# An S5, gMLP and attention layer on one core: the taps of all octaves ahead of the scan

## The chip, the cores and the metric

The kernel runs on one core of one Trainium2 chip. The metric is the device time of one execution in microseconds (us). Before the change three runs took 903.1, 904.47 and 906.89 us; their median, 904.47, is "the time before".

## The reference, cut to what matters

One encoder layer on 512 tokens of 1024 features: two mixers side by side (an S5 state space and a gMLP with spatial gating), merged by sigmoid gates, then cross-attention to 256 memory tokens, then a SwiGLU feed-forward part. The change touches the S5 branch alone:

```python
u = xa.reshape(seq, 32 groups, 16 channels)
y = d * u
for direction, reverse in ((0, False), (1, True)):
    lam_bar = exp(lam * step)                       # (32 groups, 64 states), complex
    bu = einsum('gpc,lgc->lgp', b_bar, u)
    states = scan(s[l] = lam_bar * s[l-1] + bu[l])  # over 512 positions
    y += einsum('gcp,lgp->lgc', c, states).real
y = gelu(y)
ya = y * sigmoid(y @ w_glu)
...
merged = gate_a * (ya @ w_proj_a) + gate_b * (yb @ w_proj_b)
```

## The kernel before, in words

**Main stream.** TensorE runs one product after another. Every weight block is loaded by SP (tile `wraw`, some blocks ahead of use), then split into two parts by ScalarE (`whi`, L85) and VectorE (`wlo`, L86), and each product is made of three partial ones. In order: the first half of zv (`tokm`), xa for S5 (`feat`), the second half of zv, gate A, the spatial mixing (`sv`), zu, gate B, then fourteen products with `w_proj_b` in the form of a 2x2 scheme with seven products for each half of the columns (tiles `bx`, `bq`, `qv`, L1193 to L1228), and then `finish_side()`, the GLU product of S5 (`w_glu`, four blocks deep, tile `pf`), `w_proj_a`, `w_out` and the rest. Sums of weight blocks that the 2x2 schemes need are made by DMA in DRAM: SP copies a block (L274), POOL adds another onto it (L275; tiles `bsum`, `qsum`, `dsum`).

**S5 as a side program.** `s5_program` (L955) is a Python generator that issues S5's instructions between those of the main stream. After each weight block the main stream calls `tick(us)` with the block's nominal time (5.2 us for a block of `w_in`, 2.7 for a pair product). A tick adds 0.8 of that time to a credit; while there is credit the generator is run on, and each `yield x` uses up x of it. `yield None` gives the credit back and waits for the next tick. `later(n, f)` has f issued n units of 5.2 us later. So the program order is paced by ticks. Which instruction an engine takes next is then settled by the framework's scheduler, in program order as far as data and buffers are ready; it may bring an instruction forward a long way. Instructions given to `in_order` keep their order among themselves. At run time every engine works its list strictly in order.

**What S5 computes.** The 512 positions are cut into 64 chunks of Q = 8, the 32 groups into four *octaves* of 8.
- `s5_setup` makes powers of lam_bar (`pe`, `pw`, `ca`, `cb`) and the scaled b and c (`raw_c`).
- `s5_kernels(o)` (L781) makes the *factors* of octave o, e0 and e1 (c times powers; 128 x 1024 numbers each; six VectorE operations, L790 to L797), then from them the *taps* inside a chunk: `products` fills `bd` (L804, L807) and multiplies (`pk`, L814, L819), `store` copies them to `ks` (L829) and adds d (L830), `spill` writes them to DRAM (`kd`, L837, L838), and `load` reads them back in Toeplitz form with eight DMAs (`tt`, L845). The factors have two buffers for each of e0 and e1, and tt has one.
- `s5_inputs(o)` (L853) makes the input factors in `wsx` on VectorE, turns them (`pw`), multiplies them with u (`pz`) and keeps the result in `zh` (L878, L879).
- `s5_scan` (L895) runs the recurrence over 62 chunks on VectorE, four small operations a step (L900 to L903).
- `s5_outputs(o)` (L906) copies the shifted states to `ss` (POOL memsets L916 and L917, ScalarE copies L918 and L919, the lower and the upper half of the partitions, for the real and the imaginary part apart), multiplies u with tt and ss with e0 and e1 (`mix_`, tile `py`, L929), copies the sum to `y` (`emit`), turns it (`turn_y`, `pyt`), applies gelu (`put`, L947) and stores y to DRAM (`yd`, L950): one half of the partitions through SP's queue and the other through POOL's.

**The order around the change.** `s5_program` runs the setup, the factors and taps of octaves 0 and 1, the four inputs, the scan, and then outputs 0, factors and taps 2, outputs 1, factors and taps 3, outputs 2, outputs 3. `ks` and `y` share one buffer (tag "y"). At the end `finish_side()` (L1229) issues what is left, the S5 pool is closed (L1230) and a pool `merge` takes its memory. In it lie `ygt`, which reads the four yd back (L1240), and the operands `yg_hi` and `yg_lo` of the GLU product (L1241); `pad` (L130) and the loads of gate A (`gat`, L1263) come there too.

Of the kernel before, what the change touches and what calls it, by code (L numbers as in the profile page):

```python
# [9 lines left out]
F32 = mybir.dt.float32  # L10
# [7 lines left out]
P = 128  # L18
# [8 lines left out]
G = 32  # L27
C = 16
# [11 lines left out]
Q = 8  # L40
NCH = T // Q
NO = 4
GO = G // NO
# [9 lines left out]
def hybrid_layer_kernel(  # L53
# [8 lines left out]
    nc = tc.nc  # L62
# [9 lines left out]
    dp = ctx.enter_context(tc.tile_pool(name="scratch", bufs=1, space=DRAM))  # L72
# [370 lines left out]
    def later(n, fn):  # L443

        side["later"].append((side["now"] + n, fn))
# [103 lines left out]
    s5p = s5.enter_context(tc.tile_pool(name="s5", bufs=1))  # L549
# [47 lines left out]
    ss = row_sums(xt[:, 1, :])  # L597
    for t in range(1, NT):
        rms_scale(xt[:, t, :], g_mix, xt[:, t, :], ss)
        if t == 1:  # L600
            ss = row_sums(xt[:, 2, :])
# [4 lines left out]
        if t == 2:  # L606
            ss = ss3
# [8 lines left out]
    st = {}  # L616
    V = nc.vector
    lo_, hi_ = slice(0, 64), slice(64, 128)

    def s5_setup():  # L620
# [13 lines left out]
        for i, src in enumerate((s5_lam_re, s5_lam_im)):  # L634
# [3 lines left out]
            l = small()  # L638
# [15 lines left out]
        for n in range(2):  # L654
# [2 lines left out]
                nc.tensor.transpose(ps[:, k, :], rows[:, :, 8 * n + k], ident[:2 * G, :2 * G])  # L657
            A_.copy(bb.rearrange("p i g c -> p c (i g)")[:, 8 * n:8 * n + 8, :], ps)
            yield None
        cc = s5p.tile([P, 2, G, C], F32, name="raw_c")  # L660
        for i in range(2):
            ps = aux("pbc", (P, C // 4, P))
            for k in range(C // 4):
# [7 lines left out]
        stp, a, rho, th, n, sn, hs, cs = (small() for _ in range(8))  # L671
# [106 lines left out]
    def glc(t):  # L778
        return t.rearrange("p g a b -> p (g a b)")

    def s5_kernels(o):  # L781

        gs = slice(o * GO, (o + 1) * GO)
        cr, ci = st["c"]
        pr, pi = st["pe"]
        es = []
        for i in range(2):
            e = s5p.tile([P, GO, Q, C], F32, tag="e%d" % i, name="e%d" % i, bufs=2)
            w = s5p.tile([P, GO, Q, C], F32, tag="etmp", name="etmp")
            V.tensor_tensor(e, outer(cr, gs, Q), inner((pr, pi)[i], gs, C), ALU.mult)  # L790
            yield 1.1
            V.tensor_tensor(w, outer(ci, gs, Q), inner((pi, pr)[i], gs, C), ALU.mult)
            yield 1.1
            if i == 0:
                V.tensor_tensor(e, e, w, ALU.subtract)
            else:
                V.scalar_tensor_tensor(glc(e), glc(e), -1.0, glc(w), ALU.mult, ALU.subtract)  # L797
            es.append(e)
            yield 1.1
        def products():  # L800
            bd = []
            for i in range(2):
                t = s5p.tile([P, GO, 2, C], F32, tag="bd", name="bd", bufs=2)
                nc.gpsimd.memset(t, 0.0)  # L804
                for d in range(2):
                    hf = slice(64 * d, 64 * d + 64)
                    nc.scalar.copy(t[hf, :, d, :], st["b"][i][hf, gs, :])  # L807
                bd.append(t)
            ps = aux("pk", (P, 2, P))
            for q in range(2):  # L810
                for i in range(2):
                    for j in range(4):
                        g = 4 * q + j
                        in_order(nc.tensor.matmul(ps[32 * j:32 * j + 32, q, :], bd[i][:, g].rearrange("p d c -> p (d c)"),  # L814
                                                  lc(es[i], g), start=(i == 0), stop=False, tile_position=(0, 32 * j)))
                for i in range(2):
                    for j in range(4):
                        g = 4 * q + j
                        in_order(nc.tensor.matmul(ps[32 * j:32 * j + C, q, 0:C], bd[i][:, g, 1, :],  # L819
                                                  es[i][:, g, Q - 1, :], start=False, stop=(i == 1),  # L820
                                                  tile_position=(0, 32 * j)))
            later(0.5, lambda: store(ps))

        def store(ps):
            ks = s5p.tile([P, 2, P], F32, tag="y", name="ks")
            dd = s5p.tile([P, 2, C], F32, tag="dd", name="dd", bufs=2)
            in_order(V.tensor_tensor(dd, st["dmask"].unsqueeze(1).to_broadcast([P, 2, C]),
                                     st["dcol"][:, 2 * o:2 * o + 2].unsqueeze(2).to_broadcast([P, 2, C]), ALU.mult))
            nc.scalar.copy(ks, ps)  # L829
            V.tensor_tensor(ks[:, :, 0:C], ks[:, :, 0:C], dd, ALU.add)  # L830
            later(0.5, lambda: spill(ks))

        def spill(ks):
            kd = dp.tile([GO, C, 15, C], F32, name=f"kd{o}")
            for j in range(4):
                kdj = kd.rearrange("(q j) c l e -> j c q (l e)", j=4)[j]
                (nc.gpsimd, nc.sync)[o > 1].dma_start(kdj[:, :, 7 * C:15 * C], ks[32 * j:32 * j + C])  # L837
                nc.gpsimd.dma_start(kdj[:, :, 0:7 * C], ks[32 * j + C:32 * j + 2 * C, :, 0:7 * C])  # L838
            later(1.2, lambda: load(kd))

        def load(kd):
            tt = s5p.tile([P, GO, P], F32, tag="tt", name="tt")
            kf = kd.rearrange("g c l e -> c g (l e)")
            for l in range(Q):
                (nc.gpsimd, nc.sync)[o > 1].dma_start(tt[l::Q], kf[:, :, (7 - l) * C:(15 - l) * C])  # L845
            st["oct", o] = (es[0], es[1], tt)

        later(1, products)
        yield 0.1

    turned = set()

# [53 lines left out]
    def s5_outputs(o):  # L906
        gs = slice(o * GO, (o + 1) * GO)
        while ("oct", o) not in st:
            yield None
        e_re, e_im, tt = st["oct", o]  # L910
        zh, u = st["zh"], st["u"]
        ss = s5p.tile([P, 2, GO, NCH], F32, tag="wt", name="ss", bufs=2)
        ss = (ss[:, 0], ss[:, 1])
        for i, s in enumerate(ss):
            zv = zh[:, :, i, gs].rearrange("p n g -> p g n")
            nc.gpsimd.memset(s[lo_, :, 0:1], 0.0)  # L916
            nc.gpsimd.memset(s[hi_, :, NCH - 1:NCH], 0.0)  # L917
            nc.scalar.copy(s[lo_, :, 1:NCH], zv[lo_, :, 0:NCH - 1])  # L918
            nc.scalar.copy(s[hi_, :, 0:NCH - 1], zv[hi_, :, 0:NCH - 1][:, :, ::-1])  # L919

        def mix_():
            ps = aux("py", (P, 4, 2, 4, C))
            for h in range(4):
                for k in range(3):
                    for j in range(2):
                        g = 4 * j + h
                        a = u[:, o * GO + g, :] if k == 0 else ss[k - 1][:, g, :]
                        b = (tt[:, g, :], lc(e_re, g), lc(e_im, g))[k]
                        in_order(nc.tensor.matmul(ps[64 * j:64 * j + 64, :, :, h, :].rearrange("p q d c -> p d q c"), a,  # L929
                                                  b.rearrange("p (d q c) -> p d q c", d=2, q=4),  # L930
                                                  start=k == 0, stop=k == 2, tile_position=(0, 64 * j)))
            later(1, lambda: emit(ps))

        def emit(ps):

            y = s5p.tile([P, 512], F32, tag="y", name="y")
            nc.scalar.copy(y, ps.rearrange("p q d g c -> p (q d g c)"))
            later(0.5, lambda: turn_y(y))

        def turn_y(y):  # L940
            ps = aux("pyt", (P, 2, 4, NCH))
            for q in range(4):
                in_order(nc.tensor.transpose(ps[:, :, q, :], y[:, q * P:(q + 1) * P], ident))
            later(0.5, lambda: put(y, ps))

        def put(y, ps):
            nc.scalar.activation(y, ps.rearrange("p s q n -> p (s q n)"), AF.Gelu_apprx_tanh)  # L947
            ydo = yd[o].rearrange("(s f) (d q) n -> d f s (q n)", s=2, d=2)
            for d in range(2):
                (nc.sync, nc.gpsimd)[d].dma_start(ydo[d], y[64 * d:64 * d + 64].rearrange("p (s r) -> p s r", s=2))  # L950

        later(0.5, mix_)
        yield 0.1

    def s5_program():  # L955
        yield from s5_setup()
        yield from s5_kernels(0)
        yield from s5_kernels(1)
        while "u" not in st:
            yield None  # L960
        zh = s5p.tile([P, NCH, 2, G], F32, name="zh")
        st["zh"] = zh
        for o in range(NO):
            yield from s5_inputs(o)
        while st.get("nz", 0) < 2 * NO:
            yield None
        yield None
        yield from s5_scan()
        for _ in range(2):
            yield None  # L970
        for o in range(NO):
            yield from s5_outputs(o)
            if o + 2 < NO:
                yield from s5_kernels(o + 2)

    def finish_side():
        while side["gen"] is not None or side["later"]:
# [25 lines left out]
    u = s5p.tile([P, G, NCH], F32, tag="u", name="u")  # L1003
# [179 lines left out]
    for q, ts in ((5, T1), (6, T0)):  # L1183
        for i in range(2):
            k = slice(2 * i, 2 * i + 2)
# [641 lines left out]
```

## Time and profile before

| | |
|---|---|
| three runs, median (lowest, highest) | 904.47 us (903.1, 906.89) |
| the profiled execution, its own time | 905.0 us |
| its span, first to last instruction | 903.2 us |
| mean granted clock of TensorE | 0.985 |
| TensorE busy | 867.9 us, 96% |
| VectorE, ScalarE, POOL busy | 643.8, 486.0, 102.2 us |
| HBM | 157.61 MB read, 46.63 MB written |

How to read the lines further down. A wait line names the engine and line that waited, what it waited for, and the total, the number and the longest wait in us. A line of the chain gives the start, the duration and the work that the end hung on. A windows line gives a stretch, its length, each engine's busy time in it (with the instructions), the granted clock (PEclk, 1.00 is full), the busy share of the DMA engines and GB/s. A time line's row gives start, duration, engine, line, operation, output<-input and shape, and in brackets the idle time ahead of it with what ended it. A group's row gives the count and min/median/max in ns, or the busy time in us and the mean in ns. A DMA row gives the count, the size of one and the median us from issue to landing. "SPq" and "POOLq" are those engines as issuers of DMAs.

### The profile page before, as it was taken

How to read it: one execution, taken by the hardware profiler on the slowest of the kernel's cores; microseconds unless marked ns; L12 is line 12 of the kernel's file. 1: busy time of each engine (PE TensorE's matmuls, PEld its weight loads, DVE VectorE, ACT ScalarE, POOL GpSimd, SP SyncE). 2: the span in 40 equal slices, each digit the busy share in tenths (PEclk: the TensorE clock that was granted, in tenths of full speed). 3: DMA queues.
4: the chain of work that ended last, by engine and by line, in shares of the span. 5: the costliest groups of instructions: out<-in, count | busy, mean ns of one | idle time of the engine just before them, and what ended most of it. 6: DMA issues, size and time to landing. Idle time of an engine off the chain costs nothing.

```text
span 903.2 us, 14797 instructions
## 1 busy us (share of the span) xinstructions
PE 867.9 (96%) x5760; PEld 771.5 (85%) x5760; DVE 643.8 (71%) x1048; ACT 486.0 (54%) x716; POOL 102.2 (11%) x153
## 2 busy tenths in 40 slices
PE   9999999999996939999999999999999999999996
PEld 6788888888796828889989978999999999988875
DVE  5698545898585435758856845776778777899875
ACT  5646974343585323446656634655554554665664
POOL 1005201111021110001001101101111111000010
PEclk9999999999998969999999999999999999999999
DMA  8677367878334794663469738428799999356672
GB/s 260 185 207 200 92 191 187 195 181 197 104 95 137 233 260 116 224 207 116 162 207 283 193 115 209 141 54 228 168 258 234 216 226 251 95 163 208 200 229 98
DMA packets 116360, 165.36 MB, mean 183 GB/s; under 512 B 9393, under 2 KB 82241, under 8 KB 116162
## 3 DMA queue, kind: packets, MB, share of 16 engines
q1 hardware_dynamic: 95746, 135.74, 46.3%
q0 software_dynamic: 20256, 28.15, 19.3%
q8 instruction: 45, 0.74, 0.3%
q10 hardware_dynamic: 288, 0.52, 0.2%
q14 instruction: 25, 0.20, 0.1%
HBM read 157.61 MB, written 46.63 MB: 226 GB/s over the span
## 4 chain that ended last, share of the span: by engine, by line
PE 88%; DMA 5%; ACT 3%; issue 2%; DVE 1%; SPq 1%; POOLq 0%; POOL 0%; ACTq 0%; DVEq 0%
PE pf L358 25%; PE pt L358 17%; PE px L1128 12%; PE pq L1128 6%; PE dx L358 5%; PE dq L358 3%; PE pv L1128 3%; PE qx L1128 2%; PE bx L1128 2%; PE dv L358 2%; PE pz L873 2%; DMA yd<-y 1%; PE psc L358 1%; PE qq L1128 1%; PE ptr L520 1%
## 5 line engine op out<-in xcount | busy, mean ns | idle before, releaser
L86 DVE TENSOR_TENSOR wlo<-wraw,whi 128x1024 fp32r<-128x1024 f32 (+1 forms) x145 | 172.3, 1189 | 94.9 <-ACT whi L85 91.1
L85 ACT CAST whi<-wraw 128x1024 fp32r<-128x1024 f32 (+1 forms) x145 | 148.4, 1026 | 155.6 <-PE pf L358 43.9
L358 PE MATMUL pf<-xn,whi 128*128 128x512 f32 x448 | 139.3, 392 | 0.0
L358 PEld LDWEIGHTS pf<-xn,whi 128*128 128x128 f32 x448 | 83.5, 188 | 17.2 <-issue 0.3
L358 PE MATMUL pf<-xn,wlo 128*128 128x512 f32 x224 | 87.4, 390 | 0.0
L1128 PE MATMUL px<-fn,whi 128*128 128x256 f32 x480 | 83.3, 277 | 0.0
L1128 PEld LDWEIGHTS px<-fn,whi 128*128 128x128 f32 x480 | 72.5, 188 | 0.2
L85 ACT CAST whi<-b 128x1024 fp32r<-128x1024 f32 x40 | 42.2, 1054 | 50.7 <-PE px L1128 27.7
L86 DVE TENSOR_TENSOR wlo<-b,whi 128x1024 fp32r<-128x1024 f32 x40 | 48.9, 1223 | 27.3 <-ACT whi L85 27.3
L1128 PE MATMUL px<-fn,wlo 128*128 128x256 f32 x240 | 66.4, 277 | 0.0
L1128 PE MATMUL pq<-s,whi 128*128 128x256 f32 x320 | 55.0, 276 | 0.0
L358 PE MATMUL dx<-whi,s 128*128 128x512 f32 x170 | 53.4, 391 | 0.4 <-DVE h L1752 0.4
L85 ACT CAST whi<-t 128x1024 fp32r<-128x1024 f32 x30 | 31.6, 1054 | 35.3 <-PE pv L1128 12.4
L86 DVE TENSOR_TENSOR wlo<-t,whi 128x1024 fp32r<-128x1024 f32 x30 | 36.7, 1225 | 19.4 <-ACT whi L85 19.4
L358 PEld LDWEIGHTS pf<-xn,wlo 128*128 128x128 f32 x224 | 42.0, 188 | 8.9 <-issue 0.2
L1128 PEld LDWEIGHTS pq<-s,whi 128*128 128x128 f32 x320 | 48.2, 188 | 0.0
L1128 PEld LDWEIGHTS px<-fn,wlo 128*128 128x128 f32 x240 | 45.1, 188 | 0.0
L1128 PE MATMUL pq<-s,wlo 128*128 128x256 f32 x160 | 44.2, 276 | 0.0
L358 PE MATMUL pt<-whi,xn 128*128 128x512 f32 x128 | 43.5, 410 | 0.4 <-ACT xn L85 0.4
L358 PEld LDWEIGHTS dx<-whi,s 128*128 128x128 f32 x170 | 31.8, 188 | 7.5 <-issue 0.8
L275 POOL DMA_DIRECT2D dsum<-in_w_down_dram x12 | 13.2, 1103 | 177.0 <-DMA dsum<-in_w_down_dram 176.6
L358 PE MATMUL dx<-wlo,s 128*128 128x512 f32 x85 | 33.0, 391 | 0.2 <-DVE wlo L86 0.2
(454 smaller groups left out, 2237.9 us busy)
## 6 DMA issues: line engine op xcount, KB each, us to landing
wraw<-in_w_in_dram SPq DMA_DIRECT2D x36, 512.0 KB, 4.5
dsum<-in_w_down_dram SPq DMA_DIRECT2D x20, 512.0 KB, 5.1
wraw<-dsum SPq DMA_DIRECT2D x20, 512.0 KB, 4.2
b<-in_w_gate_dram SPq DMA_DIRECT2D x15, 512.0 KB, 5.2
b<-in_w_up_dram SPq DMA_DIRECT2D x15, 512.0 KB, 4.6
wraw<-in_w_down_dram SPq DMA_DIRECT2D x15, 512.0 KB, 4.2
dsum<-in_w_down_dram POOLq DMA_DIRECT2D x10, 512.0 KB, 7.0
dsum<-dsum POOLq DMA_DIRECT2D x10, 512.0 KB, 7.4
```

The lines of the kernel that those rows point to most:

```text
L85: hi = nc.scalar.copy(dst_hi, src)
L86: lo = nc.vector.tensor_tensor(dst_lo, src, dst_hi.bitcast(F32), ALU.subtract)
L275: plan[j + step][1].append((0, lambda d=dst, x=more: nc.gpsimd.dma_start(d, x, accum_op=ALU.add)))
L358: m = nc.tensor.matmul(ps, a[x], b[y], start=start and i == 0, stop=stop and i == 2, skip_group_check=free)
L520: nc.tensor.transpose(ps[:, j, :], src[:, k * P:(k + 1) * P], ident)
L873: nc.tensor.matmul(ps[:, g, :], wt[:, g, :], u[:, o * GO + g, :], start=True, stop=True)
L1128: nc.tensor.matmul(ps[:, j, :], a[x], b[y], start=start and j == k == i == 0, stop=k == 3 and i == 2, skip_group_check=True)
```

## The change

Taps of all four octaves are made ahead of the scan: `s5_program` makes octaves 2 and 3 where 0 and 1 were, and 0 and 1 after the inputs. As there are two buffers for the factors, those of octaves 2 and 3 are stored to DRAM (`ed`) and read back by `reload`, half a unit after the mix whose buffer they take. `tt` alternates between two buffers, one of them that of `raw_c`. `ks` moves from y's buffer to that of `bd`. All kd stores of the first kind, all tt loads and both halves of y go through SP's queue. The copies to `ss` become one on ScalarE and one on VectorE; the mix begins with e0 and e1 and ends with tt; it is issued one unit after the copies and not half a unit, and each output uses 5.0 of credit and not 0.1.

```diff
-        cc = s5p.tile([P, 2, G, C], F32, name="raw_c")
+        cc = s5p.tile([P, 2, G, C], F32, tag="raw_c", name="raw_c")
...
         def products():
+            if o in ed:
+                for i in range(2):
+                    nc.sync.dma_start(ed[o][i], glc(es[i]))
...
         def store(ps):
-            ks = s5p.tile([P, 2, P], F32, tag="y", name="ks")
+            ks = s5p.tile([P, 2, P], F32, tag="bd", name="ks", bufs=2)
...
-                (nc.gpsimd, nc.sync)[o > 1].dma_start(kdj[:, :, 7 * C:15 * C], ks[32 * j:32 * j + C])
+                nc.sync.dma_start(kdj[:, :, 7 * C:15 * C], ks[32 * j:32 * j + C])
                 nc.gpsimd.dma_start(kdj[:, :, 0:7 * C], ks[32 * j + C:32 * j + 2 * C, :, 0:7 * C])
-            later(1.2, lambda: load(kd))
-
-        def load(kd):
-            tt = s5p.tile([P, GO, P], F32, tag="tt", name="tt")
-            kf = kd.rearrange("g c l e -> c g (l e)")
-            for l in range(Q):
-                (nc.gpsimd, nc.sync)[o > 1].dma_start(tt[l::Q], kf[:, :, (7 - l) * C:(15 - l) * C])
-            st["oct", o] = (es[0], es[1], tt)
+            st["kd", o] = kd
+            if o not in ed:
+                later(1.2, lambda: load(o, es))
...
+    ed = {o: dp.tile([2, P, GO * Q * C], F32, name=f"ed{o}") for o in (2, 3)}
+
+    def load(o, es):
+        tt = s5p.tile([P, GO, P], F32, tag=("tt", "raw_c")[o % 2], name="tt")
+        kf = st["kd", o].rearrange("g c l e -> c g (l e)")
+        for l in range(Q):
+            nc.sync.dma_start(tt[l::Q], kf[:, :, (7 - l) * C:(15 - l) * C])
+        st["oct", o] = (es[0], es[1], tt)
+
+    def reload(o):
+        es = [s5p.tile([P, GO, Q, C], F32, tag="e%d" % i, name="e%d" % i, bufs=2) for i in range(2)]
+        for i, e in enumerate(es):
+            nc.sync.dma_start(glc(e), ed[o][i])
+        load(o, es)
...
-        ss = (ss[:, 0], ss[:, 1])
-        for i, s in enumerate(ss):
-            zv = zh[:, :, i, gs].rearrange("p n g -> p g n")
-            nc.gpsimd.memset(s[lo_, :, 0:1], 0.0)
-            nc.gpsimd.memset(s[hi_, :, NCH - 1:NCH], 0.0)
-            nc.scalar.copy(s[lo_, :, 1:NCH], zv[lo_, :, 0:NCH - 1])
-            nc.scalar.copy(s[hi_, :, 0:NCH - 1], zv[hi_, :, 0:NCH - 1][:, :, ::-1])
+        zv = zh[:, :, :, gs].rearrange("p n i g -> p i g n")
+        nc.gpsimd.memset(ss[lo_, :, :, 0:1], 0.0)
+        nc.gpsimd.memset(ss[hi_, :, :, NCH - 1:NCH], 0.0)
+        nc.scalar.copy(ss[lo_, :, :, 1:NCH], zv[lo_, :, :, 0:NCH - 1])
+        V.tensor_copy(ss[hi_, :, :, 0:NCH - 1], zv[hi_, :, :, 0:NCH - 1][:, :, :, ::-1])
...
-                for k in range(3):
+                for k in (1, 2, 0):
...
-                                                  start=k == 0, stop=k == 2, tile_position=(0, 64 * j)))
+                                                  start=k == 1, stop=k == 0, tile_position=(0, 64 * j)))
             later(1, lambda: emit(ps))
+            if o + 2 in ed:
+                later(0.5, lambda: reload(o + 2))
...
-                (nc.sync, nc.gpsimd)[d].dma_start(ydo[d], y[64 * d:64 * d + 64].rearrange("p (s r) -> p s r", s=2))
-
-        later(0.5, mix_)
-        yield 0.1
+                nc.sync.dma_start(ydo[d], y[64 * d:64 * d + 64].rearrange("p (s r) -> p s r", s=2))
+
+        later(1, mix_)
+        yield 5.0
...
         yield from s5_setup()
-        yield from s5_kernels(0)
-        yield from s5_kernels(1)
+        for o in (2, 3):
+            yield from s5_kernels(o)
...
         for o in range(NO):
             yield from s5_inputs(o)
+        for o in (0, 1):
+            yield from s5_kernels(o)
...
         for o in range(NO):
             yield from s5_outputs(o)
-            if o + 2 < NO:
-                yield from s5_kernels(o + 2)
```

More of the change, by code (lines that the diff above doesn't have):

```diff
@@ L923, in mix_ @@
             for h in range(4):
-                for k in range(3):
+                for k in (1, 2, 0):
                     for j in range(2):
                         g = 4 * j + h
-                        a = u[:, o * GO + g, :] if k == 0 else ss[k - 1][:, g, :]
+                        a = u[:, o * GO + g, :] if k == 0 else ss[:, k - 1, g, :]
                         b = (tt[:, g, :], lc(e_re, g), lc(e_im, g))[k]
```

## The prediction

> **What bounds the kernel now.** I read the page's totals first, then the list of what TensorE waited for, then the chain that ended last around the largest wait, then the stages by windows, and last the engines' time lines there.
>
> ```profile
> span 903.2 us, 14797 instructions
> PE 867.9 (96%) x5760; PEld 771.5 (85%) x5760; DVE 643.8 (71%) x1048; ACT 486.0 (54%) x716; POOL 102.2 (11%) x153
> PE pf L358 <- ACT yg_hi L85: 15.5, 1, 15.5
> PE bx L1128 <- ACT whi L85: 3.7, 1, 3.7
> PE bx L1128 <- ACT u L1146: 3.1, 1, 3.1
> PE py L929 <- DMA tt<-kd: 2.2, 1, 2.2
> ```
>
> TensorE is busy 867.9 of 903.2 us, so a change pays only through the 35.3 us in which TensorE stands, or through TensorE's clock. Four waits hold 15.5 + 3.7 + 3.1 + 2.2 = 24.5 of them, and all four lie in S5's output stage or at its end.
>
> ```profile
> 311.11 6.99 DMA qsum<-qsum
> ...
> 319.35 10.21 DMA yd<-y
> ...
> 330.59 3.12 DMA ygt<-yd
> ...
> 333.91 0.63 ACT yg_hi L85
> ...
> 334.58 35.58 PE pf L358 x144
> ```
>
> The last product of the pair stage ends at 319.1 us. Its successor, the GLU product (pf), needs ygt, which needs yd, and the half of the last y that POOL stores lands only 10.21 us after its issue at 319.35: POOL's queue first held a qsum addition. Then come the read back (3.12), a cast and the restart.
>
> ```profile
> core 0: us, PE busy (x) PEld busy (x) DVE busy (x) ACT busy (x) POOL busy (x), PEclk, DMA share, GB/s
> 240.00:262.00 22.00, 21.66 (x203) 17.94 (x201) 11.62 (x14) 21.62 (x25) 4.66 (x12) 1.00 0.26 72
> 271.00:280.00 9.00, 2.14 (x11) 1.64 (x10) 7.29 (x9) 6.88 (x9) 2.44 (x5) 0.74 0.40 109
> 280.00:308.00 28.00, 27.93 (x308) 27.22 (x307) 12.74 (x15) 12.00 (x17) 3.41 (x7) 0.96 0.59 180
> 312.00:319.00 7.00, 7.00 (x70) 6.71 (x66) 1.92 (x2) 2.13 (x3) 0.32 (x1) 1.00 0.74 252
> 319.00:334.60 15.60, 0.10 (x2) 0.02 (x1) 2.56 (x4) 1.73 (x3) 2.87 (x4) 0.63 0.99 282
> 334.60:340.20 5.60, 5.60 (x13) 4.40 (x14) 2.55 (x4) 2.96 (x4) 0.00 (x0) 0.51 1.08 308
> ```
>
> The granted clock (PEclk) says what a wait costs afterwards. After the 15.5 us it is 0.51 for 5.6 us, a loss of 5.6 x 0.49 = 2.7 us. After the two waits of 3.7 and 3.1 it is 0.96 over 28 us (1.1 us lost), and the last 0.8 us of the window before ran at half (0.4): 1.5 together. The wait of 2.2 at 308 to 312 leaves 1.00 behind it.
>
> **The change, part by part.** All prices are set against the profiled execution, 905.0 us (span 903.2, 1.8 around it); the median of the three runs, 904.47, is 0.5 below it.
>
> *Octaves 2 and 3 leave the output stage.* Their taps are made there now, between the outputs.
>
> ```profile
> L790 DVE TENSOR_TENSOR e<-raw_c,pe 128x1024 f32<-128x1024 f32 x4 | 4.7, 1220 | 0.0
> L918 ACT COPY ss<-zh x8: 1077/1124/1143, 241.6 to 269.4; 64x504 f32<-64x504 f32 x8
> 272.36 1.28 ACT L947 ACT_TABLE_LOAD   x1
> 273.66 0.60 ACT L947 ACTIVATE y<-pyt 128x512 f32<-128x512 f32 x1
> 274.15 1.99 ACT L85 CAST whi<-wraw 128x1024 fp32r<-128x1024 f32 x2
> 277.30 0.37 ACT L829 COPY ks<-pk 128x256 f32<-128x256 f32 x1 [1.17 <-DMA yd<-y]
> ```
>
> An octave is six such VectorE operations, so 12 x 1.22 = 14.6 us of VectorE leave this stage, with eight small bd copies and two of ks on ScalarE, pk's products on TensorE (moved, not saved) and eight stores of kd each on SP and POOL. The two waits of 3.7 and 3.1 go with them: the cast that ends the first (274.15) stands behind four ss copies, a table load and a gelu; the second is lengthened by ks, which waits 1.17 us for y's store because ks shares y's buffer. In the change ks takes bd's buffer.
>
> *They arrive ahead of the scan.* Octaves 2 and 3 take the place that 0 and 1 had; 0 and 1 are made after the inputs.
>
> ```profile
> 122.58 1.23 DVE L792 TENSOR_TENSOR etmp<-raw_c,pe 128x1024 f32<-128x1024 f32 x1
> 121.00:150.00 29.00, 29.00 (x165) 24.51 (x165) 9.03 (x18) 16.29 (x20) 3.35 (x7) 1.00 0.72 178
> 149.72 0.23 DVE L900 TENSOR_TENSOR sa<-zh,ca 128x64 f32<-128x64 f32 x1 [2.61 <-ACT zh L879]
> L903 DVE TENSOR_TENSOR zh<-sa,sb x62: 215/225/227, 150.3 to 240.0; 128x64 f32<-128x64 f32 x62
> ```
>
> The third row is a window like those above: VectorE works 9.03 of 29 us between the inputs' last factors and the scan's first step, which waits for zh. 20 us are free, and 14.6 fit. The pacing agrees: counting the kernel's ticks, the scan's first step falls on the same block of gate A in both, since the new taps stand where the program now waits for zh. I cost this at nothing; without that cover it is at most 14.6 us on a chain that, below, has more slack than that.
>
> *SP's queue.* Ahead of the scan SP gets 4 stores of ed, 16 issues of kd and 16 of tt; POOL loses 8 and 16.
>
> ```profile
> L837 SPq DMA_DIRECT2D kd<-ks x8: 414/423/456, 278.0 to 297.7; - x8
> L845 SPq DMA_DIRECT2D tt<-kd x16: 537/598/624, 284.0 to 307.6; - x16
> wraw<-bsum SPq DMA_DIRECT2D x8, 512.0 KB, 3.6
> tt<-kd SPq DMA_DIRECT2D x16, 64.0 KB, 2.5
> yd<-y SPq DMA_DIRECT2D x4, 128.0 KB, 2.6
> yd<-y POOLq DMA_DIRECT2D x4, 128.0 KB, 3.6
> ```
>
> That is 16 x 0.42 + 16 x 0.6 + 4 x 0.4 = 18 us of issuing, over some 100 us in which a weight block is wanted every 5.2 us by the kernel's own ticks, and three are on their way. What queues behind a tt load that waits for its kd are weight loads. The kernel does the same now at 284 to 308, with a block every 2.7 us, and TensorE stands there only for py. Cost nothing; without the cover one landing (2.5 to 3.6 us) an octave.
>
> *The read back.* New in the output stage: two loads of 512 KB for e an octave, ahead of the tt loads that were there. Issue per octave is 2 x 0.4 + 8 x 0.6 = 5.6 us, landing 3.6 more. The loads wait for mix 0 and mix 1, whose buffers they take, and weight loads queue behind them on SP. DMA has room: its share is 0.26 in 240 to 262. Mix 2 waits in TensorE's fixed order for them: between 0 and 9.2 us an octave, 18.4 in all; the nearest row is the present wait of py for tt, 2.2. I take **2 us** for both.
>
> *ss copies.* Four of 1.1 us an octave on ScalarE become one there of 64x1008 (between 1.1 and 2.2; 2.1, since a whi cast of 128x1024 takes 1.0 and a gelu of half of that 0.6) and one on VectorE (1.2 by a 128x1024 operation; at most 2.2). ScalarE goes from 17.7 to 8.4 us, VectorE gains 4.8. But the four gelus now fall between gate B's last sigmoids: up to four more table loads of 1.28 us. S5's work on ScalarE, 8.4 + 4.8 (y's copies and gelus, eight of 0.6) + 1.3 to 6.4, must pass in some 28 us beside its casts and sigmoids. Those took 21.6 - 12 x 1.1 - 0.6 = 7.8 of the 22 us from 240 to 262 (12 of the 16 copies and one y lie there), so 10 of 28: together 24 to 30 us. It may be late by 0 to 5 us (four table loads in one burst); I take **2**.
>
> A rule of the Trainium skill speaks against this part: "ScalarE: Activation LUTs", What ACT_TABLE_LOAD costs, gives 2.66 us for a switch, as half of it is a drain behind the load. The row above shows the gelu 0.02 us after the load's end, so no drain is seen; by the rule four switches would be 10.6 us and I would put 5 in place of 2.
>
> *y by SP and the end.* Two stores of 0.6 us on SP, landing in 2.6, replace the one that took 10.21 us.
>
> ```profile
> L947 ACT ACTIVATE y<-pyt x4: 586/597/601, 273.7 to 316.8; 128x512 f32<-128x512 f32 x4
> L1240 SPq DMA_DIRECT2D ygt<-yd x4: 326/424/430, 329.7 to 331.1; - x4
> ```
>
> More matters the order: outputs run straight on (5.0 of credit apart), and from the first output's start to the fourth gelu I count 6.0 pacing units of 5.2 us against 9.7 now, 18.9 us less. The fourth gelu ran at 316.8; by that shift it runs at 298, and by the data alone (240.0, 8.4 of copies, 18.4 of reads back, some us of mixes) near 270. Gelu, two issues, landing, read and cast are 0.6 + 1.2 + 2.6 + 3.5 + 0.6 = 8.5 us, so yg is there by 307 at the latest. The last product will end about 319.1 - 6.8 - 1.5 - 2.2 + 4 = 312.6. So yg is ready first, and the 15.5 us go with the 2.7 behind them. Next late are the weights: DMA moved 282 GB/s in the gap, and much of that must now pass under products.
>
> **Sum:** 905.0 - 15.5 - 2.7 - (3.7 + 3.1) - 1.5 - 2.2 + 2 + 2 = **880**.
>
> A second rule only shifts cents: "TensorE: Matmul & The Clock Gate", Part 1, has the clock back after about 3.4 us of work; here it took 5.6. By the rule the restart was worth 1.7, and the sum would be 881.
>
> **The rivals.** (a) *ScalarE stays the bound at the seam* of gate B and the pair products: 21.62 of 22 us busy now, and nearly the same work pressed into a like stretch. Then the three small waits stay as they are (24.5 - 15.5 + 1.5 = 10.5 us with their clock) and only the end is won: 905.0 - 18.2 = 887, and up to 892 with all the table loads. For it: the sum of 24 to 30 us above. Against it: VectorE loses 14.6 - 4.8 = 10 us of work there, and 12 copies fell on ScalarE by 262 while TensorE worked 21.66 of 22 us.
>
> (b) *The change doesn't do what it says at the end*: yg's reads stay behind the last product, held by S5's memory (all four reads were issued from 329.7 to 331.1, behind the last store, though three y's were there before) or by SP's order. Then only the queue is won: the last halves land at 317.4 + 1.2 + 2.6 = 321.2 and not 329.6, with 905.0 - 8.4 = 897. Against it: that memory is free when the fourth store is done, and the program's order is no bar, since taps of octave 2 ran at 122.6, far ahead of their place.
>
> (c) *Slower: the read back holds TensorE.* Mix 2 and 3 keep their place in TensorE's order; if that place comes before ten DMAs on SP behind mix 0 have landed, TensorE stands, the weights behind them on SP are late too, and the clock halves. At 72 to 180 GB/s the 1.5 MB of an octave take 8 to 21 us; 15 us twice with 2.7 us of clock each are 35 against the 28.7 + 2 won without new waits: 905.0 - 28.7 + 35 + 2 = 913. It decides once both waits together pass 30 us. For it: one such wait is in the trace. Against it: that one is 2.2 us, and the loads start while a mix and gate B's products still run.
>
> **How the numbers follow.** Forecast 880, between 872 (no new wait, and something of the remaining idle time) and 886: 0.55. Rival (a) 887 to 892: 0.20. Rival (b) 897: 0.12, rival (c) 913: 0.09. Some mixture that ends within 0.5% of the time before, which is about what a measurement of this kernel can tell from no change: 0.04. So faster by over 0.5% (below 900) 0.86, with a small part of (b) outside; same 0.05; slower 0.09. The range from 872 to 897 takes in (a) and most of (b). Against the median it is 880 for 904.5.
>
> **What would show it.** In the changed profile: the wait of pf L358 for yg_hi gone or under 2 us, with ygt's reads issued before the last bq product; no granted clock of 0.5 between 260 and 340; the first scan step within 3 us of 149.7 and the last within 5 of 240; no L790 after the scan; py waiting under 3 us for e or tt; table loads between 240 and 275, one to five. The prediction is wrong if the scan starts late, if py waits for the e loads, or if ygt is read only after the products.

## The result, and the profile after

The changed kernel takes 880.98 us (median of four runs, 879.08 to 881.58), the kernel before 905.01 beside it: a ratio of 0.9731 [0.9705, 0.9757]. The forecast was 880. The profiled run took 881.58 us (before: 905.0).

The page's totals after the change:

```profile
span 879.8 us, 14794 instructions
PE 863.4 (98%) x5760; PEld 766.9 (87%) x5760; DVE 648.0 (74%) x1052; ACT 479.4 (54%) x706; POOL 85.8 (10%) x117
```

TensorE's idle time fell from 903.2 - 867.9 = 35.3 us to 879.8 - 863.4 = 16.4, and its busy time fell by 4.5 with the same 5760 matmuls, which is the clock. (The page's mean clock went from 0.985 to 0.998, but that mean takes in stretches in which TensorE stands, such as the 15.6 us at 0.63 before, so it can't be multiplied with the busy time.) 18.9 + 4.5 = 23.4 us is the whole change of the span. The sum on record had 20.5 of idle time (24.5 less the 4 it added) and 4.2 of clock.

What TensorE waited for in the changed kernel (total, times, longest in us):

```profile
PE pw L879 <- ACT zh L892: 2.1, 1, 2.1
PE pyt L956 <- ACT y L950: 1.4, 1, 1.4
PE pk L817 <- ACT bd L810: 1.2, 1, 1.2
...
PE bx L1141 <- ACT zf L1230: 0.6, 1, 0.6
...
PE bq L1141 <- ACT whi L85: 0.2, 1, 0.2
```

The 15.5 of pf, both waits of bx on ScalarE and the 2.2 of py are gone. 2.1 + 1.4 + 1.2 + 0.6 = 5.3 us came, the largest of them ahead of the scan, where I had costed everything at nothing.

The end of the pair products and the start of the GLU product, as windows with the same columns as those of before:

```profile
300.00:314.40 14.40, 13.51 (x115) 13.09 (x115) 10.72 (x14) 7.77 (x10) 0.00 (x0) 1.00 0.87 303
314.40:320.00 5.60, 5.60 (x27) 4.61 (x26) 4.26 (x5) 3.22 (x4) 0.85 (x1) 1.00 0.96 306
```

The GLU product begins at 314.4 and TensorE goes into it at full clock; before, the 5.6 us behind the gap ran at 0.51. The chain that ended last shows why it doesn't wait:

```profile
291.15 4.67 DMA yd<-y
...
297.34 5.00 DMA ygt<-yd
...
302.36 0.62 ACT yg_hi L85
...
314.45 25.63 PE pf L358 x113
```

The last half of y leaves at 291.15 and yg is cast at 303.0, 11.5 us ahead of its product. Both transfers are slower than I took them (4.67 and 5.00 against 2.6 and 3.5). DMA moves 268 GB/s from 291.0 to 302.5; whether that is why was not tested. It costs nothing.

### The profile page after: what moved, and what is told of

Its sections match the earlier page's. It is cut to its first block, busy times and chain, and to the rows that moved or that the text cites. A ratio compares the mean times of both kernels' runs of the same rounds, so it can differ in the third digit from the quotient of the medians.

```text
span 879.8 us, 14794 instructions
## 1 busy us (share of the span) xinstructions
PE 863.4 (98%) x5760; PEld 766.9 (87%) x5760; DVE 648.0 (74%) x1052; ACT 479.4 (54%) x706; POOL 85.8 (10%) x117
## 4 chain that ended last, share of the span: by engine, by line
PE 79%; DMA 7%; ACT 4%; DVE 4%; issue 3%; SPq 2%; POOL 1%; POOLq 0%; ACTq 0%; DVEq 0%
PE pf L358 22%; PE pt L358 14%; PE px L1141 12%; PE pq L1141 6%; PE dx L358 5%; PE dq L358 3%; PE pv L1141 3%; PE qx L1141 2%; DVE wlo L86 2%; PE dv L358 2%; DMA yd<-y 1%; PE psc L358 1%; PE qq L1141 1%; PE ptr L520 1%; ACT whi L85 1%
## 5 line engine op out<-in xcount | busy, mean ns | idle before, releaser
L358 PEld LDWEIGHTS pt<-whi,xn 128*128 128x128 f32 x128 | 24.3, 193 | 6.7 <-ACT xn L85 1.2
```

The lines of the kernel that those rows point to most:

```text
L358: m = nc.tensor.matmul(ps, a[x], b[y], start=start and i == 0, stop=stop and i == 2, skip_group_check=free)
```

## The experiments

**Theory.** The end is a race between S5's chain (last y, store, read, cast) and the pair products. The change wins it by the order of S5's work, wins the small waits at the seam with ScalarE, and y's one queue is only a help. **Rivals:** the gain is that of a single edit (the queue, the buffer of ks, the ss copies), and moving the taps adds nothing; or the read back has a price that the sum left out. Ratios are to the kernel before on the same chip (medians 906.86, 908.02 and 907.14 us for the three groups), with 95% intervals; 0.01 is about 9 us. The changed kernel was not run again in these groups; its 0.9731 stands beside 905.01. Each experiment computes the same result; in the two scan experiments the added operation multiplies by ones.

### One small edit at a time, in the kernel before

*Both halves of y through SP:*

```diff
-                (nc.sync, nc.gpsimd)[d].dma_start(ydo[d], ...
+                nc.sync.dma_start(ydo[d], ...
```

> The kernel before, with both halves of y stored through SP's queue and nothing else changed. Theory (the order of S5 carries the gain): only the slow landing of the last half on POOL's queue goes, the last y comes as late as before, so the wait of pf for yg_hi falls from 15.5 to about 7 us and the time to 897. Rival (the queue alone held the end): the wait falls under 2 us and the time to 887.

Measured: 900.75 us, 0.9926 [0.9899, 0.9953], so 6.7 us less. Its largest wait:

```profile
PE pf L358 <- ACT yg_hi L85: 9.5, 1, 9.5
```

15.5 became 9.5. The queue's share of the gap is what the prediction's rival (b) had priced (8.4), a little less; the greater part of the gap is not the queue.

*ks in bd's buffer:*

```diff
-            ks = s5p.tile([P, 2, P], F32, tag="y", name="ks")
+            ks = s5p.tile([P, 2, P], F32, tag="bd", name="ks", bufs=2)
```

> The kernel before, with ks in bd's buffer and nothing else changed. Theory: ScalarE's two waits of 2.2 us for y's store go, of which TensorE feels at most one; 902 to 905, the end as before. Rival (ks behind y's store is what stops TensorE at 271 to 279): both waits of 3.7 and 3.1 us and their clock go, 897.

Measured: 889.04 us, 0.979 [0.9749, 0.9831]: 19 us from one line, which neither side expected. Before, the last product of octave 2's taps ended early (time line of TensorE):

```profile
261.83 0.28 PE L819 MATMUL pk<-e,bd 128*16 128x16 f32 x16
```

and the copy of it into ks ran at 277.30, 15 us later, though its row names an idle time of only 1.17. With the edit (time lines of TensorE and ScalarE):

```profile
265.90 0.28 PE L819 MATMUL pk<-e,bd 128*16 128x16 f32 x16
266.28 0.37 ACT L829 COPY ks<-pk 128x256 f32<-128x256 f32 x1
```

The copy follows its product by 0.1 us. Sharing y's buffer, ks had to come behind the first output's gelu (273.66, a row of the prediction) and the store of that y, for which its own row waits. What stood ahead of that gelu in ScalarE's order was other work (four ss copies, casts, a table load), which shows as busy time and not as a wait. What TensorE waits for with the edit, the largest first:

```profile
PE bx L1128 <- ACT whi L85: 4.0, 1, 4.0
PE pyt L943 <- ACT y L937: 1.9, 1, 1.9
```

The 15.5 of pf and the 3.1 of u are gone, the 3.7 of whi stands at 4.0, and small waits of 1.9 and less are new. In the profiled runs TensorE stands 21.9 us in place of 35.3 and works 865.8 in place of 867.9, so the span is 15.5 shorter; the 19 is from the ratio, whose interval is 15 to 23. POOL's issues show the order turned round:

```profile
312.14 0.60 POOL L950 DMA_DIRECT2D yd<-y  x1 [14.26 <-ACT y L947]
330.40 1.22 POOL L275 DMA_DIRECT2D qsum<-in_w_q_dram  x1 [14.92 <-DMA qsum<-qsum]
```

y's half now goes out ahead of the qsum addition that had held it back.

*One ss copy on ScalarE and one on VectorE* (the change's own lines for ss, put into the kernel before):

```diff
-            nc.scalar.copy(s[lo_, :, 1:NCH], zv[lo_, :, 0:NCH - 1])
-            nc.scalar.copy(s[hi_, :, 0:NCH - 1], ...)          # both in a loop over s (real, imaginary)
+        nc.scalar.copy(ss[lo_, :, :, 1:NCH], zv[lo_, :, :, 0:NCH - 1])
+        V.tensor_copy(ss[hi_, :, :, 0:NCH - 1], ...)
```

> The kernel before, with one ss copy on ScalarE and one on VectorE an octave, in place of four on ScalarE, and nothing else changed. Theory: ScalarE loses 9 us of work at the seam, so the wait of 3.7 us for the cast goes with part of its clock, 899 to 902, the end as before (pf still waits over 12 us). Rival (the taps' 14.6 us on VectorE are what make the casts late): no change, 904 to 906.

Measured: 899.93 us, 0.9915 [0.9886, 0.9943]. TensorE's waits:

```profile
PE pf L358 <- ACT yg_hi L85: 18.3, 1, 18.3
PE py L927 <- DMA tt<-kd: 2.0, 2, 1.4
PE bx L1126 <- ACT u L1144: 1.3, 1, 1.3
```

The 3.7 is gone and the 3.1 is 1.3. The products end 6.4 us earlier (312.6 for 319.1) and S5's chain only 3.7 (pf starts at 330.9 for 334.6), so pf waits 18.3 in place of 15.5.

*All three together:*

> The kernel before with the three small edits together (both halves of y through SP, ks in bd's buffer, two ss copies an octave), the taps of octaves 2 and 3 still made between the outputs. Theory: the small edits give the queue's 8 us and part of the seam's 8 us, so 888 to 892, and 7 to 11 us are left for the order. Rival (the order matters little, the small edits carry the gain): 881 to 883, like the changed kernel.

Measured: 893.4 us, 0.9847 [0.9803, 0.9891]. The edits alone are worth 6.7 + 19 + 7.7 = 33 us by their ratios; together they give 14, and no more than ks alone. That is above both ranges. TensorE's two largest waits:

```profile
PE pf L358 <- ACT yg_hi L85: 3.7, 1, 3.7
PE py L927 <- DMA tt<-kd: 3.6, 1, 3.6
```

In the old order the end still waits, and so does the last mix for its taps. What the changed kernel has beyond these three edits (0.9731 against 0.9847, some 10 us) is the order of the taps with what comes with it: the read back, the mix's order and its pacing.

*ks and the queue without the ss copies:*

> The kernel before with ks in bd's buffer and both halves of y through SP, the ss copies as before. Theory: with ks free S5's end is early enough that the queue adds nothing, 0.977 to 0.983 of the time before, as with ks alone (0.979). Rival (y through SP is what made the three small edits slower together than ks alone): 0.984 to 0.988, with yd's two issues and tt's loads in each other's way on SP.

Measured: 894.35 us, 0.9869 [0.9836, 0.9903], behind ks alone by 0.008, with intervals that barely part: in this order one queue for y takes some 7 us by the ratios, as the rival had it. SP's time line:

```profile
296.89 4.40 SPq L845 DMA_DIRECT2D tt<-kd  x7
301.39 1.25 SPq L950 DMA_DIRECT2D yd<-y  x2
...
311.03 1.24 SPq L950 DMA_DIRECT2D yd<-y  x2
```

The third y, ready at about 295, waits behind the tt loads of the last octave, and the last leaves at 311. This is what the rival named, but it is not shown to be the cause. The copy of the last y (306.0) waits for its own mix, and yg is cast at 318.8, as with ks alone (318.7). The products end 2.6 us earlier than there, so pf waits 1.6; then it waits 3.2 for ya, behind the GLU product, with a clock of 0.72 for the 6 us after. Why that wait is there was not followed. So the same edit gains 6.7 us in the kernel before and loses about 7 beside the edit of ks, and only the gain is explained.

### One part taken back, in the changed kernel

*y by SP and POOL again* (the reverse of the first edit):

> The changed kernel with y's halves on SP and POOL again. Theory: the last y is stored some 23 us ahead of the last product's end and yg is cast about 11 us ahead, so even a landing of 10 us on POOL's queue is hidden: 881 to 884, pf waits under 3 us. Rival (the queue carries the end): 889 and more, with a wait of pf of 8 us.

Measured: 885.31 us, 0.9757 [0.9728, 0.9786]; the interval overlaps that of the changed kernel, and pf does not wait. *ks in y's buffer again:*

> The changed kernel with ks in y's buffer again. Theory now (ks in y's buffer held the taps of octaves 2 and 3 behind the outputs, so it costs only where taps are made between outputs; with all taps ahead of the scan it no longer matters): 0.970 to 0.978 of the time before, like the changed kernel's 0.973, and pf doesn't wait. Rival (ks's buffer is by itself what the change won): 0.985 to 1.0, and pf waits 8 us or more.

Measured: 882.11 us, 0.9728 [0.9699, 0.9757]. The line worth 19 us in the old order is worth nothing in the new one. What it does move is the scan, by its last operation of each step (column: first to last start in us):

```profile
L916 DVE TENSOR_TENSOR zh<-sa,sb x62: 215/225/228, 151.2 to 240.8; 128x64 f32<-128x64 f32 x62
```

and the waits of pw and pk ahead of it are gone. So with all taps ahead of the scan neither the queue nor the buffer is needed by itself. No run takes both back or moves the taps and nothing else, and the mix's new order and pacing were not tried alone.

*Four ss copies on ScalarE again:*

> The changed kernel with the four ss copies an octave on ScalarE again. Theory: 9 us more of ScalarE work fall on gate B and the first pair products; S5's end moves by some 4 us, inside its 11 us of slack, and TensorE loses 0 to 5 us to late casts: 881 to 886. Rival (the ss copies are what made the waits at 271 to 279): 889 and more.

Measured: 889.93 us, 0.9807 [0.9783, 0.9831], clear of the changed kernel's interval: 7 us. Waits, and a window at the seam:

```profile
PE py L942 <- DMA e<-ed: 2.9, 2, 2.4
...
PE bq L1143 <- ACT whi L85: 1.4, 1, 1.4
```

```profile
268.00:276.00 8.00, 6.56 (x42) 5.75 (x44) 3.70 (x6) 7.89 (x11) 0.00 (x0) 0.57 0.77 217
```

ScalarE works 7.89 of 8 us, TensorE stands 1.44 and runs at 0.57: 6.56 x 0.43 = 2.8 us of clock and 1.4 of standing in this window alone. It is rival (a)'s place, but the stop ahead of the slow clock is rival (c)'s: py stands 2.41 us, up to 269.44, for the read back of e. ScalarE is what starts it: a weight's cast stands behind eight ss copies until 258.71 and its second part ends at 261.02; SP, which waits for that buffer, issues the next weight load at 261.04 and the loads of e behind it, at 261.46 and not at 256.74. The ss edit kept that away.

### The race delayed on purpose

One more VectorE operation in every step of the scan, then three:

```diff
             V.tensor_tensor(b, zh[:, n - 1, ::-1, :], st["cb"], ALU.mult)
+            V.tensor_tensor(b, b, ones[...], ALU.mult)      # once, and three times
```

> The changed kernel with one more VectorE operation in each of the scan's 62 steps (b is multiplied by ones, so the result stays). Theory (S5's end is a race against the last product, won by some 11 us): the scan ends 10 to 16 us later, which is about the slack, so the time stays within 881 to 888 and pf waits 0 to 6 us. Rival (S5's end is no longer tied to the time at all): 881 to 882 here and in the next run.

Measured: 883.92 us, 0.9749 [0.9721, 0.9777]. SP's stores of y (column: first to last issue):

```profile
L964 SPq DMA_DIRECT2D yd<-y x8: 580/598/1162, 284.4 to 308.8; - x8
```

S5 ends 17.6 us later (308.8 for 291.2), the GLU product starts 2.3 later (316.6), pf waits 0.5, and no change from the changed kernel is shown.

> The same with three more operations a step. Theory: the scan ends 30 to 48 us later, 20 to 37 us over the slack; pf waits that long less what is already lost at the seam, and the clock halves behind it: 900 to 920. Rival (not tied): 881 to 884.

Measured: 938.3 us, 1.0335 [1.0304, 1.0367]. The scan ends at 324.6, 78 us later and far more than expected: one added operation cost 14.6 us over 62 steps, 0.24 each, three cost 0.42 each. Why the price rises was not followed. TensorE's waits and the stores:

```profile
PE py L943 <- DVE ss L933: 25.9, 1, 25.9
PE pyt L959 <- ACT y L953: 9.5, 3, 4.5
PE pf L358 <- ACT yg_hi L85: 7.4, 1, 7.4
```

```profile
L966 SPq DMA_DIRECT2D yd<-y x8: 574/606/630, 344.7 to 362.2; - x8
```

The time is outside the range too. Now the mixes, fixed in TensorE's order, stand for the scan, and pf waits again. The last y leaves 71.0 us later, the GLU product (368.3) only 54.0: from the last issue to that product it is 23.3 us in the changed kernel and 6.1 here. The difference, 17 us, is the cover that S5's end has. The first run bears it out: 17.6 us of delay left a wait of 0.5. Read from the profile alone the cover was 11.5; but the store and the read, 4.67 and 5.00 us in the changed kernel, take 2.41 and 2.74 here, where nothing is left to cover them.

### Disputed costs by themselves

*A second buffer for y* (`tag=("y", "etmp")[o % 2]`):

> The changed kernel with y in two buffers by turns (the second is that of the factors' work tile, which is free by then). Theory: S5's end comes some 8 us earlier, which is worth nothing since yg is early already, and only TensorE's wait of pyt for y (1.4 us) goes: 0.970 to 0.974 of the time before. Rival (y's single buffer still holds ScalarE's queue and with it the casts): 0.965 to 0.969.

Measured: 879.29 us, 0.9709 [0.9684, 0.9734]. The wait of pyt is gone, as expected; a gain over the changed kernel is not shown, the intervals overlap.

*Each read back issued twice:*

```diff
         for i, e in enumerate(es):
-            nc.sync.dma_start(glc(e), ed[o][i])
+            for _ in range(2):
+                nc.sync.dma_start(glc(e), ed[o][i])
```

> The changed kernel with each of the four e loads issued twice, so that the read back moves 2.1 MB more through SP's queue. Theory (the read back is nearly hidden): py waits 1 to 4 us more for e and S5's end moves by 4 to 8 us inside its slack, 0.973 to 0.979 of the time before. Rival (the read back is what the change pays with): 0.982 and more, with waits of py for e of 8 us or more.

Measured: 894.41 us, 0.9837 [0.9803, 0.987], about 10 us more than the changed kernel: the rival's time, but not its wait of 8 us for e. TensorE's waits, and SP's weight loads around the read back:

```profile
PE pyt L957 <- ACT y L951: 4.2, 3, 2.3
PE bq L1142 <- ACT whi L85: 3.3, 1, 3.3
...
PE py L941 <- DMA e<-ed: 2.2, 1, 2.2
```

```profile
258.06 0.37 SPq L224 DMA_DIRECT2D wraw<-in_w_proj_b_dram  x1
...
281.45 0.54 SPq L224 DMA_DIRECT2D wraw<-bsum  x1
```

23.4 us pass on SP without a weight load. The same place in the changed kernel:

```profile
255.20 0.37 SPq L224 DMA_DIRECT2D wraw<-in_w_proj_b_dram  x1
256.74 0.91 SPq L861 DMA_DIRECT2D e<-ed  x2
257.70 5.88 SPq L855 DMA_DIRECT2D tt<-kd  x8
...
272.05 0.54 SPq L224 DMA_DIRECT2D wraw<-bsum  x1
```

16.9 us without one, and TensorE does not stand. In the doubled run too none of the three waits named is traced to a weight that came late. The 2.2 of py is for e; the 4.2 of pyt is for copies of y, which wait 2.1 to 5.2 us for the store of the y before; the 3.3 of bq, at 312 to 315, is for a cast that stands on ScalarE behind one of yg, which waits 2.33 us for ygt. S5's last store leaves 12.3 us later (303.5), not 4 to 8. The waits named above, 9.7 us, are of the size of the loss, but the changed kernel has a wait of pyt too, and which part is the queue and which the transfers was not told apart.

## Why the prediction was right, and where it was not

- **The end (15.5 + 2.7).** Right in mechanism and size: a race, won by the order. The delayed scans show the race, and taking back the queue or ks's buffer, one at a time, leaves it won; the three small edits in the old order do not win it (pf waits 3.7). But the order is not the only way: ks alone won it too. The fourth gelu ran at 289.8 (I bounded it by 298; 9.7 less 6.0 units of 5.2 are 19.2 us, not the 18.9 on record, which leaves the bound), yg was ready at 303.0 (by 307), the last product ended at about 314 (312.6), the reads of yd were issued at 296.0 to 297.3, ahead of the last pair products. Rival (b) did not come: S5's memory was free in time.
- **The two waits on ScalarE (3.7 + 3.1, 1.5 of clock).** Read rightly: the ss copies alone take the first away, ks's buffer alone the second. What I had wrong was the price of sharing that buffer, taken as part of a 3.1 wait with 1.17 us of it on a store. It held octave 2's taps and the outputs behind them back (counted from the scan's end, the last gelu comes 9.7 us earlier without it), and alone it was worth 19 us [15 to 23], as much as the whole gap with its clock. The sum came out since the reorder removes the same waits; they have more than one sufficient cure. That was luck as far as ks goes: had the change been that edit alone, I should have been wrong.
- **Taps ahead of the scan at nothing.** This step failed. The scan's last operation of a step, from the changed kernel:

```profile
L916 DVE TENSOR_TENSOR zh<-sa,sb x62: 216/225/227, 157.9 to 246.8; 128x64 f32<-128x64 f32 x62
```

  It starts 7.6 us late and ends 6.8 late, outside both limits on record and so a sign of being wrong that the prediction had named, and TensorE loses 2.1 + 1.2 us at pw and pk. VectorE's room, on which I rested, was not what ran out. The first step of the scan waits for ScalarE:

```profile
157.40 0.23 DVE L913 TENSOR_TENSOR sa<-zh,ca 128x64 f32<-128x64 f32 x1 [2.28 <-ACT zh L892]
```

  The cause is ks in bd's buffer: with y's buffer both waits and the delay go, while in the four other runs that take the changed kernel's bd buffer and leave the scan as it is, that last operation starts for the last time between 245.5 and 250.6. Part of the way can be read. POOL's clearing of bd now waits in two places, 5.6 us in all, for the stores of kd, which read ks; with y's buffer it never does. The next octave's ks is copied at 93.95, against 84.64 with y's buffer, and the first copy of zh, in the same list of ScalarE, comes at 95.43 against 86.54. How that leads to the wait ahead of the scan was not followed. The 17 us of cover paid for the delay of the scan, not for the 3.3 us at pw and pk.
- **The read back at 2.** No wait of py for e or tt stands in the changed kernel, so 0 and not 2; doubled, it costs about 10. Rival (c)'s wait of mix 2 for e is there in small in two runs, 2.2 us with the read back doubled and 2.9 with four ss copies on ScalarE; this change doesn't reach it.
- **ss and ScalarE late by 2.** The copies, with min/median/max in ns:

```profile
L929 ACT COPY ss<-zh x4: 1971/1996/2050, 248.8 to 259.6; 64x1008 f32<-64x1008 f32 x4
L930 DVE COPY ss<-zh x4: 1049/1080/1094, 247.0 to 259.6; 64x1008 f32<-64x1008 f32 x4
```

  2.0 and 1.08 us against the 2.1 and 1.2 taken. Of the up to four more table loads two came by 280. The lateness is 1.4 at pyt and 0.2 at bq, near the 2. The rule on a drain behind the load ("ScalarE: Activation LUTs", What ACT_TABLE_LOAD costs, in the Trainium skill) is again not seen, in ScalarE's time line:

```profile
261.62 1.28 ACT L960 ACT_TABLE_LOAD   x1
262.91 0.60 ACT L960 ACTIVATE y<-pyt 128x512 f32<-128x512 f32 x1
```

  The gelu starts 0.01 us behind the load.
- **SP's queue at nothing.** Right as far as weights go: of TensorE's two waits ahead of the scan none is for a weight. SP issues the first stores of kd at 78.87, behind the last store of ed (73.42, 4.72 us); whether that has a part in the scan's delay was not tested.
- **y by SP.** "More matters the order" was right: taken back in the new order it shows no difference. In the old order the same line is worth +6.7 alone and about -7 beside the edit of ks.
- **The sum.** New waits 5.3 against 4, so 880 against 880.98. That these two are so near is luck: 3.3 of the 5.3 come from the step put at nothing, and the read back, put at 2, cost nothing.

## What to carry to other kernels

Where a schedule is laid out ahead of time, a shared buffer shows as order and hardly as a wait: measure from the producer's end to the consumer's start (15 us here), not the idle time in front of the consumer (1.17). A gap at a place where two chains meet is one race, so what shortens the late chain past its cover earns nothing more, and edits that each close it must not be added up. Delaying the chain that should be early, in known steps, measures its cover: 17 us here, where the profile read by itself gave 11.5.

## What the runs showed of the hardware

A short stop has a price that varies. TensorE stands 2.07 of 3.5 us at the same product, pw, in the changed kernel and in that with two buffers for y. The changed kernel, then the other (windows, PEclk third from the end):

```profile
110.00:113.50 3.50, 1.43 (x9) 1.21 (x9) 0.29 (x1) 3.44 (x5) 0.45 (x1) 1.00 0.21 78
113.50:117.00 3.50, 3.50 (x17) 2.86 (x16) 3.43 (x4) 3.46 (x5) 0.00 (x0) 1.00 0.61 225
```

```profile
112.00:115.50 3.50, 1.43 (x9) 0.96 (x8) 0.06 (x1) 3.45 (x4) 0.55 (x1) 1.00 0.29 105
115.50:119.20 3.70, 3.70 (x11) 2.90 (x10) 3.61 (x4) 3.65 (x5) 0.00 (x0) 0.54 0.55 195
```

The first goes on at 1.00, the second at 0.54 for 3.7 us, a loss of 1.7. The Trainium skill ("TensorE: Matmul & The Clock Gate", Part 1) has the clock fall after an idle window of about 3.4 us and calls the window free-running; an idle time of 2.07 that is followed by a lower clock in one run and not in the other does not follow from that window alone. The profiled run of the second took 884.5 us where its median is 879.29; how much of that is such windows was not measured, but a difference of this size is not to be read from two traces.
